# The last head of a Q·Kᵀ kernel stored in two halves, the first one by a scattering GpSimd DMA that leaves eight partitions to two small stores

## The chip, the cores and the metric

The kernel runs on one core of a Trainium2 chip. The metric is the device time of one execution in microseconds (us). Before the change it is 1061.1 us, the median of three runs (1060.9 to 1062.3).

A core has a matrix engine (TensorE, PE in the profile), a vector engine (DVE), a scalar engine (ACT), GpSimd (POOL) and a synchronisation engine (SP). Data moves between the memory outside the core (HBM, "dram" in names) and the on-chip memory SBUF by sixteen DMA engines, which work off queues. Here SP issues the stores and the early loads of q, ACT the other loads. Matrix products land in PSUM, from where ACT or DVE copies them to SBUF.

## What is computed

For each of 8 · 12 = 96 heads the kernel multiplies a 1024 x 64 matrix q with the transpose of a 1024 x 64 matrix k. The result is 96 matrices of 1024 x 1024 in 32-bit floats, 402.65 MB in all, against 50.33 MB of input.

```python
def reference(q: np.ndarray, k: np.ndarray) -> np.ndarray:
    return np.einsum('bhid,bhjd->bhij', q, k).astype(np.float32)
```

## The kernel before, in words

Synchronisation is written out by hand in one critical section, so the order of instructions on each engine is the order in which the Python code issues them. `Engine.run` (L33) gives an instruction its semaphore waits and one increment; `Landing.start` (L53) adds 16 to a semaphore when a DMA has landed.

Heads are worked through in blocks of 2, 2, 4, 8 and then five times 16 heads. While one block's products are computed, the next block's q and k are loaded (`load`, L153), cast to 16 bits by POOL (`cast_quads`, L201) and transposed by DVE (`transpose_quads`, L222). POOL's last cast and DVE's last transpose lie some 180 us ahead of the end, because the last block needs nothing prepared behind it.

For one head, `scores` (L256) makes 1024 rows of output. Output row 8p + t belongs to partition p and slot t, so a partition holds eight consecutive rows, 32 KB. For two slots at a time PE loads 128 columns of qT as weights and multiplies with kT in two matmuls of 512 columns each (L386), which fills one of two PSUM regions of 128 x 2048 floats. ACT copies the region into one of three output buffers `o_sb` (L288). After four such copies SP issues one store of 4 MB for the head (L301). A buffer is written again only when its store, three heads ago, has landed; ACT waits for that.

The last head (number 95, counted from 0) has a function of its own, `scores_uneven` (L307). It makes rows 0 to 127 first. The products run with only 32 columns of weights, and the result goes to the first 32 partitions of `x_sb`, the input buffer that is free by then: partition p holds rows 8p to 8p + 7, and only the first 16 partitions (rows 0 to 127) are used. ACT and DVE copy in turn (L338), and SP issues four stores of four partitions each (L359, issued in L380): partitions c, c+4, c+8 and c+12 for c = 0 to 3. Then come the rows 128 to 1023 on all 128 partitions, seven rows each, in an `o_sb` buffer; ACT alone makes the four copies, and SP issues one store of 3.5 MB (L372). At the very end SP waits for the semaphores of all stores (L513).

Of the kernel before, what the change touches and what calls it, by code (L numbers as in the profile page):

```python
# [5 lines left out]

F16 = mybir.dt.float16
F32 = mybir.dt.float32
P = 128


class Engine:
# [8 lines left out]
    def missing(self, events):  # L21
        want = {}
        for counter, value in events:
            if counter is not self and value > self.seen.get(counter, 0):
                want[counter] = max(value, want.get(counter, 0))
        self.seen.update(want)
        return list(want.items())

    def wait(self, events):
        for counter, value in self.missing(events):  # L30
# [29 lines left out]
def kernel(  # L60
# [6 lines left out]
    nc = tc.nc  # L67

    B, H, S, D = q.shape
    NT = S // P  # L70
    BH = B * H
# [7 lines left out]
    NMAX = max(sizes)  # L79
    CHUNK, HALVES = 64 * 32, 3  # L80
    TURNS = (3, 4, 5, 6, 10, 11, 12, 13)
    LOADS = {0: {}, 1: {}, 2: {1: 3}, 3: {2: 1}}

    pool = ctx.enter_context(tc.tile_pool(name="sb", bufs=1))
    psum = ctx.enter_context(
        tc.tile_pool(name="ps", bufs=1, space=bass.MemoryType.PSUM)
    )
    ident = pool.tile([P, P], F16, tag="ident")
    x_sb = pool.tile([P, NMAX * S * D // P], F32, name="x_sb", tag="x")
    half_sb = [pool.tile([P, CHUNK], F16, name=f"half{i}", tag=f"half{i}") for i in range(HALVES)]  # L90
    qk_sb = [
        [pool.tile([P, NMAX * S // 2], F16, name=f"{'qk'[x]}T{i}") for x in range(2)]
        for i in range(2)
    ]
    o_sb = [pool.tile([P, NT, S], F32, name=f"o_sb{i}", tag=f"out{i}") for i in range(3)]
    ps_all = psum.tile([P, 4 * S], F32, tag="po")

    ctx.enter_context(tc.tile_critical())

    pe = Engine(nc, nc.tensor, "pe_done")  # L100
    act = Engine(nc, nc.scalar, "act_done")
    dve = Engine(nc, nc.vector, "dve_done")
    gps = Engine(nc, nc.gpsimd, "pool_done")
    sp = Engine(nc, nc.sync, "sp_done")
# [18 lines left out]
    n, at = S * D // P * 2, 8 * S // 2  # L123
# [8 lines left out]
    input_busy = []  # L132
    outs = Ring(o_sb)
    input_landing = [Landing(nc, f"x{i}_in") for i in range(2)]
    tail_landing = Landing(nc, "tail_out")
    store_landing = {id(t): Landing(nc, f"out{i}_out") for i, t in enumerate(o_sb)}

    class Block:
# [165 lines left out]
            )  # L304
            out_busy.append(store_landing[id(buf)].start(dma))

        def scores_uneven(self, n, regions, w):  # L307
            half, g = divmod(n, self.N // 2)
            cs = slice(half * D, (half + 1) * D)
            qT = self.qk[0][cs, g * S : (g + 1) * S]  # L310
            kT = self.qk[1][cs, g * S : (g + 1) * S]
            head = of[self.first + n]
            Q, more, even = 32, NT, NT - 1
            few = P // more
            first = few * more

            def product(ps, slot, stationary, at, signal):
                m = stationary.shape[1]
                pe.run(lambda: load_weights(stationary, half * D, at), signal=False)
                for j in range(2):  # L320
                    col = slot * S + j * 512
                    done = pe.run(
                        lambda: multiply(
                            ps[0][at : at + m, col : col + 512],
                            stationary,
                            kT[:, j * 512 : (j + 1) * 512],
                            half * D,
                            at,
                        ),
                        ps[1],  # L330
                        signal=signal and j == 1,
                    )
                return done

            def evacuate(ps, done, dst, parts, N, events=(), by_dve=False):
                copier = dve if by_dve else act
                copied = copier.run(
                    lambda: (nc.vector.tensor_copy if by_dve else nc.scalar.copy)(  # L338
                        out=dst, in_=ps[0][:parts, : N * S]
                    ),  # L340
                    [*events, done],
                )
                ps[2].append(copied)
                return copied

            more_sb = x_sb[:Q, : more * S]
            written = []
            for t in range(0, more, w):
                ps = regions.next()
                for tt in range(w):  # L350
                    stationary = qT[:, t + tt :][:, : Q * more - more + 1 : more]
                    done = product(ps, tt, stationary, 0, tt == w - 1)
                dst = more_sb[:, t * S : (t + w) * S]
                by_dve = t // w % 2
                written.append(evacuate(ps, done, dst, Q, w, input_busy, by_dve))
            sp.wait(written)
            dst = head[:first].rearrange("(p t) j -> p (t j)", t=more)
            for c in range(4):
                self.store_part(sp, tail_landing, dst[c::4], more_sb[c:few:4])  # L359

            buf, out_free, _ = outs.next()
            rows = qT[:, first:].rearrange("c (m t) -> c t m", t=even)
            for t in range(0, even, w):
                ps = regions.next()
                N = min(w, even - t)
                for tt in range(N):
                    done = product(ps, tt, rows[:, t + tt], 0, tt == N - 1)
                dst = buf[:, t : t + N].rearrange("p t j -> p (t j)")
                copied = evacuate(ps, done, dst, P, N, out_free)
            self.over = [done]  # L370
            sp.wait([copied])
            self.store_part(  # L372
                sp,
                store_landing[id(buf)],
                head[first:].rearrange("(p t) j -> p (t j)", p=P),
                buf[:, :even].rearrange("p t j -> p (t j)"),
            )

        def store_part(self, eng, landing, dst, src):
            landing.start(eng.eng.dma_start(out=dst, in_=src))  # L380

    def load_weights(stationary, at, to=0):
        return nc.tensor.ldweights(stationary, tile_position=(at, to))  # L383

    def multiply(dst, stationary, moving, at, to=0):
        return nc.tensor.add_instruction(  # L386
            mybir.InstMatmult(
                name=nc.get_next_instruction_name(),
                ins=[nc.tensor.lower_ap(moving), nc.tensor.lower_ap(stationary)],
                outs=[nc.tensor.lower_ap(dst)],  # L390
                start_tensor_calc=True,
                stop_tensor_calc=True,
                ldweights=False,
                tile_position=(at, to),
                tile_size=(D, stationary.shape[1]),
            )
        )

    blocks, first = [], 0
# [6 lines left out]
    at = 0  # L406
# [24 lines left out]
    for x in range(2):  # L431
# [7 lines left out]
                out=ident,  # L439
                in_=ident,  # L440
                compare_op=mybir.AluOpType.not_equal,
                fill=1.0,
                base=0,
                pattern=[[-1, P]],
                channel_multiplier=1,
# [20 lines left out]
    def block(i, heads, regions, w):  # L466
        b = blocks[i]
        nxt = blocks[i + 1] if i + 1 < len(blocks) else None
        for n in heads:
            side = {}  # L470
            if nxt and nxt.by_pe:
                if n == 1:
                    side = {
                        u: [
                            lambda x=u // 2: nxt.transpose_rows(
                                x, regions.next(), dve, nc.vector.tensor_copy
                            )
                        ]
                        for u in (1, 3)
                    }  # L480
            elif nxt:
                parts = nxt.chunks()
                at = TURNS if i > EARLY else [m * b.N // len(parts) for m in range(len(parts))]
                some = [s for m, s in zip(at, parts) if m == n]
                side = {0: [lambda s=s: transposed(nxt, s) for s in some]}
            at = LOADS.get(i, {1: 1, 7: 1})
            if n in at:
                side[at[n]] = side.get(at[n], []) + [lambda: next_load(act)]
            if i == len(blocks) - 1 and n == b.N - 1:
                b.scores_uneven(n, regions, w)  # L490
            else:
                b.scores(n, side, regions, w)
            to_half(i + 2 + (n == b.N - 1))
# [16 lines left out]
    block(0, [1], halves_ps, 2)  # L510
    for i in range(1, len(blocks)):
        block(i, range(blocks[i].N), halves_ps, 2)
    sp.wait([(c, c.count) for c in [*store_landing.values(), tail_landing]])  # L513


# [28 lines left out]
```

## Time and profile before

| | |
|---|---|
| median of three runs | 1061.1 us (1060.9 to 1062.3) |
| the profiled execution's own time | 1061.62 us |
| its span, first to last instruction | 1059.8 us |
| moved by DMA | 453.21 MB, mean 428 GB/s |
| PE busy | 707.0 us (67%) |
| ACT busy | 699.9 us (66%) |
| DVE busy | 435.4 us (41%) |
| POOL busy | 354.0 us (33%) |
| store of one head, issue to landing | 21.7 us, 95 times |
| last store (3.5 MB), issue to landing | 15.7 us |

The profile lists groups of instructions with their busy time, the mean duration of one in nanoseconds, and the idle time ahead of them with what ended it. "SPq" is the queue of instructions that SP works through, DMA issues among them. The DMA share in a stretch of time is the mean busy share of the core's sixteen DMA engines; a packet is counted in the stretch in which it starts, so very short stretches are uneven. The trace also holds a record of every single DMA packet (start, duration, size), which the views only add up.

### The profile page before, as it was taken

Reading aid. Unit: us, or ns where it says so; the run is one execution under the profiler, and the core shown is the slowest. Engines: PE = TensorE matmul, PEld = TensorE weight load, DVE = VectorE, ACT = ScalarE, POOL = GpSimd, SP = SyncE. Lnnn points to the kernel's source line nnn. Section 1 sums busy time; section 2 is a strip of 40 time slices with the busy share of each in tenths; the row PEclk is TensorE's granted clock in tenths of the full one; section 3 lists DMA queues with packets and bytes.
Section 4 is the critical chain, followed back from the end, with each engine's and each line's share of the span. In section 5 each row is a group of like instructions: output and inputs, shape, how many; then the busy total and the mean of one; then the engine's idle time right before and its main releaser. Section 6 shows DMA issues by size and latency. Waiting matters only on the chain.

```text
span 1059.8 us, 3339 instructions
## 1 busy us (share of the span) xinstructions
PE 707.0 (67%) x1582; PEld 128.3 (12%) x807; DVE 435.4 (41%) x57; ACT 699.9 (66%) x388; POOL 354.0 (33%) x206
## 2 busy tenths in 40 slices
PE   6876744957477747557765756775574777777772
PEld 1111100101011101111110111111110111111110
DVE  2995939029193009439003907600670930000000
ACT  4766655857477737567856756775674778777772
POOL 7927465055380029064005509100913700000000
DMA  9999999999999999999999999999999999999997
GB/s 376 433 436 434 431 430 431 429 425 428 433 432 433 434 424 429 432 435 432 433 420 434 430 435 435 433 430 425 433 430 429 435 430 432 434 433 433 433 433 335
DMA packets 17041, 453.21 MB, mean 428 GB/s; under 512 B 1904, under 2 KB 1904, under 8 KB 2928
## 3 DMA queue, kind: packets, MB, share of 16 engines
q1 hardware_dynamic: 15008, 410.00, 89.9%
q10 hardware_dynamic: 2016, 42.99, 9.7%
q8 instruction: 9, 0.15, 0.0%
q14 instruction: 8, 0.07, 0.0%
HBM read 50.33 MB, written 402.65 MB: 427 GB/s over the span
## 4 chain that ended last, share of the span: by engine, by line
DMA 65%; ACT 16%; PE 8%; DVE 6%; POOL 4%; issue 1%; SPq 0%; ACTq 0%
DMA out_dram<-o_sb 60%; ACT o_sb L288 15%; PE ps_all L386 7%; DVE kT L230 4%; POOL half L211 3%; DMA x_sb<-in_k_dram 2%; DMA x_sb<-in_q_dram 2%; DVE qT L230 1%; DVE x_sb L338 0%; ACT o_sb L338 0%; DMA o_sb<-in_q_dram 0%; PE ps_all L244 0%; POOL qT L182 0%; DVE kT L251 0%; ACT kT L251 0%
## 5 line engine op out<-in xcount | busy, mean ns | idle before, releaser
L386 PE MATMUL ps_all<-kT,qT 64*128 64x512 f16 (+1 forms) x1550 | 702.9, 617 | 326.8 <-ACT o_sb L288 310.0
L288 ACT COPY o_sb<-ps_all 128x2048 f32<-128x2048 f32 (+1 forms) x380 | 687.5, 1859 | 330.5 <-DMA out_dram<-o_sb 288.3
L211 POOL CAST half<-x_sb 32x2048 f16<-32x2048 f32 x176 | 332.1, 1887 | 482.1 <-DMA x_sb<-in_q_dram 304.9
L230 DVE STREAM_TRANSPOSE qT<-half 128x2048 f16<-128x2048 f16 x22 | 202.6, 9477 | 270.8 <-POOL half L211 270.8
L230 DVE STREAM_TRANSPOSE kT<-half 128x2048 f16<-128x2048 f16 x22 | 202.3, 9525 | 134.8 <-POOL half L211 134.8
L383 PEld LDWEIGHTS <-qT 64*128 64x128 f16 (+1 forms) x775 | 125.2, 162 | 900.9 <-issue 882.2
L338 DVE COPY x_sb<-ps_all 32x2048 f32<-32x2048 f32 x2 | 4.6, 2280 | 175.5 <-PE ps_all L386 175.5
L230 DVE STREAM_TRANSPOSE kT<-kT 128x1024 f16<-128x1024 f16 x2 | 9.3, 4856 | 0.0
L230 DVE STREAM_TRANSPOSE qT<-qT 128x1024 f16<-128x1024 f16 x2 | 9.2, 4786 | 0.0
L211 POOL CAST qT<-o_sb 32x1024 f16<-32x1024 f32 x8 | 8.3, 1034 | 1.1 <-DMA o_sb<-in_q_dram 0.7
L211 POOL CAST kT<-o_sb 32x1024 f16<-32x1024 f32 x8 | 8.3, 1034 | 0.5
L338 ACT COPY o_sb<-ps_all 128x2048 f32<-128x2048 f32 (+1 forms) x4 | 6.4, 1658 | 2.7 <-PE ps_all L386 2.7
L251 DVE COPY qT<-ps_all 128x1024 f16<-128x1024 f16 x2 | 2.4, 1224 | 11.1 <-PE ps_all L244 11.1
L288 DVE COPY o_sb<-ps_all 128x1024 f32<-128x1024 f32 x4 | 4.9, 1224 | 4.4 <-PE ps_all L386 4.4
L244 PE MATMUL ps_all<-ident,qT 128*128 128x128 f16 x16 | 2.1, 311 | 6.8 <-POOL qT L182 6.7
L338 ACT COPY x_sb<-ps_all 32x2048 f32<-32x2048 f32 x2 | 3.7, 1854 | 2.1 <-PE ps_all L386 2.1
L251 ACT COPY kT<-ps_all 128x1024 f16<-128x1024 f16 x1 | 1.0, 1012 | 4.8 <-PE ps_all L244 4.8
L182 POOL CAST qT<-o_sb 128x512 f16<-128x512 f32 x4 | 2.3, 612 | 3.7 <-DMA o_sb<-in_q_dram 3.7
L251 ACT ACT_TABLE_LOAD x1 | 1.3, 1283 | 2.8 <-issue 2.8
L251 DVE COPY kT<-ps_all 128x1024 f16<-128x1024 f16 x1 | 1.2, 1224 | 4.4 <-PE ps_all L244 4.4
L182 POOL CAST kT<-o_sb 128x512 f16<-128x512 f32 x4 | 2.3, 613 | 0.5 <-DMA o_sb<-in_q_dram 0.5
L244 PE MATMUL ps_all<-ident,kT 128*128 128x128 f16 x16 | 2.0, 305 | 0.7 <-ACT o_sb L288 0.7
(8 smaller groups left out, 4.0 us busy)
## 6 DMA issues: line engine op xcount, KB each, us to landing
out_dram<-o_sb SPq DMA_DIRECT2D x95, 4096.0 KB, 21.7
x_sb<-in_q_dram ACTq DMA_DIRECT2D x5, 4096.0 KB, 24.9
x_sb<-in_k_dram ACTq DMA_DIRECT2D x5, 4096.0 KB, 23.7
out_dram<-o_sb SPq DMA_DIRECT2D x1, 3584.0 KB, 15.7
x_sb<-in_q_dram SPq DMA_DIRECT2D x1, 2048.0 KB, 14.7
x_sb<-in_k_dram SPq DMA_DIRECT2D x1, 2048.0 KB, 19.9
o_sb<-in_k_dram ACTq DMA_DIRECT2D x4, 256.0 KB, 5.0
o_sb<-in_q_dram SPq DMA_DIRECT2D x4, 256.0 KB, 5.2
```

Of the source, the lines that this page charges most:

```text
L182: lambda: nc.gpsimd.tensor_copy(out=rows[:, :, h], in_=self.raw[x][:, h * n : (h + 1) * n].rearrange("p (r d) -> p r d", d=D),),
L211: lambda: nc.gpsimd.tensor_copy(out=dst[q0 : q0 + 32].rearrange("p (r d) -> p r d", d=32), in_=raw[32 * b : 32 * b + 32, c * m : (c + 1) * ...
L230: lambda: nc.vector.transpose(out=dst, in_=buf.rearrange("p (r i) -> p r i", i=32)),
L244: lambda: nc.tensor.transpose(t_ps[:, t], rows[:, t], ident),
L251: lambda: copy(out=dst, in_=t_ps.rearrange("c t m -> c m t")), [done]
L288: lambda: (nc.vector.tensor_copy if by_dve else nc.scalar.copy)(out=dst, in_=ps[:, : w * S]),
L338: lambda: (nc.vector.tensor_copy if by_dve else nc.scalar.copy)(out=dst, in_=ps[0][:parts, : N * S]),
L383: return nc.tensor.ldweights(stationary, tile_position=(at, to))
L386: return nc.tensor.add_instruction(mybir.InstMatmult(name=nc.get_next_instruction_name(), ins=[nc.tensor.lower_ap(moving), nc.tensor.lower ...
```

## The change

Only the last head changes. It is made in two halves of 512 rows, by one function `part` for both: two products of two slots each, now with four rows to a partition (row 4p + t, 16 KB a partition), the first copied by ACT and the second by DVE.

Rows 0 to 511 go to all 128 partitions of `x_sb`. They are stored by one DMA that GpSimd issues, an indirect one: it reads for each partition, from a small integer tile `place_sb`, to which 16 KB row of the output that partition's data goes. The tile is computed on GpSimd (`places`): an iota gives each partition its row number, a copy turns it into floats, eight selects overwrite the numbers of partitions 16 to 19 and 48 to 51 by one that lies outside the output, and a copy turns it back to integers. The DMA is told that a number outside the bounds is no error: these partitions are skipped. GpSimd waits for itself between these small instructions (`settle`). The eight skipped partitions are stored by SP, in two plain DMAs of four partitions each, 64 KB a piece.

Rows 512 to 1023 go to an `o_sb` buffer in the same manner and are stored by SP in one DMA of 2 MB. The wait at the end has one semaphore more, that of the two small stores.

```diff
+    def settle(self):
+        self.eng.wait_ge(self.sem, self.count)
...
+    APART = (16, 48)
...
-        def scores_uneven(self, n, regions, w):
+        def scores_split(self, n, regions, w):
...
+            T = NT // 2
+            def part(rows, dst, events, copiers):
+                copied = []
+                for t in range(0, T, w):
+                    ps, ps_free, ps_busy = regions.next()
+                    for tt in range(w):
+                        stationary = rows[:, t + tt]
+                        pe.run(lambda: load_weights(stationary, half * D), signal=False)
+                        for j in range(2):
...
+                    copier = copiers[t // w]
+                    done = copier.run(
+                        lambda: (nc.vector.tensor_copy if copier is dve else nc.scalar.copy)(
+                            out=dst[:, t * S : (t + w) * S], in_=ps[:, : w * S]
                         ),
+                        [*events, done],
                     )
...
+            first = x_sb[:, : T * S]
+            rows = qT[:, : P * T].rearrange("c (m t) -> c t m", t=T)
+            copied = part(rows, first, input_busy, (act, dve))
+            index = self.places(first=(self.first + n) * S // T)
+            gps.wait([*copied, index])
+            tail_landing.start(
+                nc.gpsimd.indirect_dma_start(
+                    out=out.rearrange("b h (m t) j -> (b h m) (t j)", t=T),
+                    out_offset=bass.IndirectOffsetOnAxis(ap=place_sb, axis=0),
+                    in_=first,
+                    in_offset=None,
+                    bounds_check=BH * S // T - 1,
+                    oob_is_err=False,
                 )
+            )
+            sp.wait(copied)
+            for p in APART:
+                dst = head[p * T : (p + 4) * T].rearrange("(m t) j -> m (t j)", t=T)
+                self.store_part(sp, rest_landing, dst, first[p : p + 4])
...
+            second = buf[:, :T].rearrange("p t j -> p (t j)")
+            rows = qT[:, P * T :].rearrange("c (m t) -> c t m", t=T)
+            copied = part(rows, second, out_free, (act, dve))
+            sp.wait(copied)
             self.store_part(
                 sp,
                 store_landing[id(buf)],
-                head[first:].rearrange("(p t) j -> p (t j)", p=P),
-                buf[:, :even].rearrange("p t j -> p (t j)"),
-            )
+                head[P * T :].rearrange("(p t) j -> p (t j)", p=P),
+                second,
+            )
+        def places(self, first):
+            gps.settle()
+            gps.run(
+                lambda: nc.gpsimd.iota(
+                    place_sb, pattern=[[0, 1]], base=first, channel_multiplier=1
+                )
+            )
+            gps.settle()
+            gps.run(lambda: nc.gpsimd.tensor_copy(out=place_f, in_=place_sb))
+            for p in APART:
+                for i in range(4):
+                    gps.settle()
+                    gps.run(
+                        lambda: nc.gpsimd.affine_select(
+                            out=place_f,
+                            in_=place_f,
+                            compare_op=mybir.AluOpType.not_equal,
+                            fill=float(2 * BH * S),
+                            base=-(p + i),
+                            pattern=[[0, 1]],
+                            channel_multiplier=1,
+                        )
+                    )
+            gps.settle()
+            done = gps.run(lambda: nc.gpsimd.tensor_copy(out=place_sb, in_=place_f))
+            gps.settle()
+            return done
...
-    sp.wait([(c, c.count) for c in [*store_landing.values(), tail_landing]])
+    sp.wait([(c, c.count) for c in [*store_landing.values(), tail_landing, rest_landing]])
```

## The prediction

> **What bounds the kernel now.** The page first. Its DMA row is full in 39 of 40 slices, and most of ACT's idle time ends when a store lands: stores set the pace, and a head costs what 4 MB take.
>
> ```profile
> DMA  9999999999999999999999999999999999999997
> L288 ACT COPY o_sb<-ps_all 128x2048 f32<-128x2048 f32 (+1 forms) x380 | 687.5, 1859 | 330.5 <-DMA out_dram<-o_sb 288.3
> out_dram<-o_sb SPq DMA_DIRECT2D x95, 4096.0 KB, 21.7
> out_dram<-o_sb SPq DMA_DIRECT2D x1, 3584.0 KB, 15.7
> out_dram<-x_sb SPq DMA_DIRECT2D x4, 128.0 KB
> ```
>
> Then the timeline of the tail (start, duration): the four small stores go out from 1036.42 on, some 1.2 us each, the last store at 1042.86.
>
> ```profile
> 1028.05 1.85 ACT L338 COPY x_sb<-ps_all 32x2048 f32<-32x2048 f32 x1 [0.18 <-PE ps_all L386]
> 1029.82 2.28 DVE L338 COPY x_sb<-ps_all 32x2048 f32<-32x2048 f32 x1 [173.59 <-PE ps_all L386]
> ...
> 1036.42 4.67 SPq L380 DMA_DIRECT2D out_dram<-x_sb  x4
> ...
> 1038.28 4.55 ACT L338 COPY o_sb<-ps_all 128x2048 f32<-128x2048 f32 x3 [0.52 <-PE ps_all L386]
> ...
> 1042.86 0.34 SPq L380 DMA_DIRECT2D out_dram<-o_sb  x1
> ```
>
> SP's waits from 1036 us on: it waits 6.4 us for head 94 (landed 1049.6), 0.4 for the small stores, 8.4 for the last store. Nothing but transfers lies behind 1042.9.
>
> ```profile
> SPq L98 <- DMA out_dram<-o_sb: 8.4, 1, 8.4
> ...
> SPq L31 <- DMA out_dram<-o_sb: 6.4, 1, 6.4
> ...
> SPq L31 <- DMA out_dram<-x_sb: 0.4, 1, 0.4
> ```
>
> Last, DMA share by stretch of the tail (the last two columns are share and GB/s). A packet of 28 KB is 1.06 us, so a share of 0.07 in one us is one packet. From 1052 the engines run dry one after another, and one packet alone starts after 1057.
>
> ```profile
> 1048.00:1052.00 4.00, 0.00 (x0) 0.00 (x0) 0.00 (x0) 0.00 (x0) 0.00 (x0) 1.00 1.00 432
> 1052.00:1053.00 1.00, 0.00 (x0) 0.00 (x0) 0.00 (x0) 0.00 (x0) 0.00 (x0) 1.00 0.80 344
> 1053.00:1054.00 1.00, 0.00 (x0) 0.00 (x0) 0.00 (x0) 0.00 (x0) 0.00 (x0) 1.00 0.47 201
> 1054.00:1055.00 1.00, 0.00 (x0) 0.00 (x0) 0.00 (x0) 0.00 (x0) 0.00 (x0) 1.00 0.33 143
> 1055.00:1056.00 1.00, 0.00 (x0) 0.00 (x0) 0.00 (x0) 0.00 (x0) 0.00 (x0) 1.00 0.40 172
> 1056.00:1057.00 1.00, 0.00 (x0) 0.00 (x0) 0.00 (x0) 0.00 (x0) 0.00 (x0) 1.00 0.20 86
> 1057.00:1058.00 1.00, 0.00 (x0) 0.00 (x0) 0.00 (x0) 0.00 (x0) 0.00 (x0) 1.00 0.07 29
> ```
>
> **Sixteen strings of packets.** The packet records behind that view, strung end to start, give sixteen strings, one per DMA engine as I read them. A head's store is eight packets of 32 KB on each, 1.213 us apiece.
> - Four strings carry the small stores, four packets of 1.213 us each. They finish head 94 at 1042.93, 1043.25, 1044.48 and 1044.88, and their last packet at 1056.3, 1056.6, 1057.8 and 1058.2.
> - Three are late: head 94 at 1046.08, 1048.07, 1049.12, the end at 1054.6, 1056.5, 1057.6. The last one's packets run about 1.22 us all along: some 5% of 32 KB packets are over 1.216 us up to 1000 us, one engine's share. The middle one lost some 1.8 us near 979, where a 16 KB instruction packet ran.
> - Nine finish head 94 by 1045.0 and end by 1053.5.
>
> So the end, 1058.2, is set by an engine with extra packets. The mean end is 1054.65, thus 3.6 us is all that any division of the same bytes could give.
>
> **The change part by part.** An engine's end is its end of head 94 plus its packets, if they are queued in time.
>
> *Supply.* Copies keep their prices: ACT 128x2048 1.87 us, DVE 2.28 (timed on 32 partitions; its 128x1024 copies take 1.22, half, so I take 2.28). First half copied by 1032.10; the second follows in the steps of before's third and fourth copies, 1031.86 to 1033.7 on ACT (buffer free: head 92 landed near 1030.1) and 1034.05 to 1036.3 on DVE. SP's two small issues start at 1032.2, 0.75 and 1.25 us as before's; behind them waits only the last store, out at 1036.5, 6.4 us earlier. That is worth nothing at the end: the late strings are in head 94 until 1046 or later. Three early strings lose their idle of about 1 us, but end first.
>
> *Index tile.* Eleven small GpSimd operations, each 0.1 us (memset 128x1) to 1.9 us (the longest cast), and a round trip of its own semaphore each: 1 to 25 us. POOL is free from 842.8, 189 us ahead: nothing. A further instruction packet may cost one engine 0.3 us; 0, as 15 of 16 engines don't decide.
>
> *Issuing the scatter.* No GpSimd DMA is in the trace. Nearest rows: SP's issue, 0.33 to 1.28 us plus about 0.9 to the first packet; POOL's longest operation 1.9. Taken at 3 us, packets from 1035. Nothing is queued behind it on POOL but the end. The late string at 1048.07 has second-half packets until 1052.9, so only 18 us more would cost anything: nothing.
>
> *Packets.* Eight of 16 KB for each half, 0.607 us each (half of 1.213): 4.85 + 4.85 = 9.70 us, against 8.50 for eight of 28 KB. The small stores' strings have two of 0.607 instead of four of 1.213: 1044.88 + 1.21 + 9.70 = 1055.8, no longer the end. The scatter's price per byte is bounded by that rate from below and by the 2 KB packets of the first loads (84 ns against 76 at that rate, 1.11 times) from above if it is cut finer: 0 to 0.5 us; taken 0, as 16 KB load packets measured 0.608 to 0.615.
>
> *Whom it spares.* Late strings: 1046.08 + 9.70 = 1055.8; 1048.07 + 9.70 = 1057.8; 1049.12 + 9.76 = 1058.9. The eight skipped partitions are one string's share of a 128-partition store. If it is the last string's, its end is 1049.12 + 4.9 = 1054.0, and 1057.8 sets the end: 1057.77 - 1058.22 = -0.45 us. If not, 1058.88 - 1058.22 = +0.66. No view says which partitions that string serves. I take the first end: a choice and not a reading, resting only on the slowness being one engine's all along, which a fixed list of partitions can meet and a passing delay could not. Both ends stay in the range.
>
> The Trainium skill ("DMA: Bandwidth & Descriptors", The descriptor swizzle) puts partitions 16 to 19 and 48 to 51 on one engine, number 4; the same page (Latency and other measured facts) calls engines 7 and 15 usually the slower ones. By that rule the spared engine is not the slow one and the time would be rival A's; the trace agrees that one engine in sixteen is slow, and can't say which.
>
> *Sum.* Landing and wind-down behind the last packet stay (1.6 us; one semaphore more is 0.03). The profiled execution is 1061.62 us, 1.8 outside its span and 0.5 above the median: -0.45 gives 1061.17 there, **1060.6 us** against the median.
>
> **Rivals.**
> A. *The slow engine isn't spared*, and the change doesn't do what the skip suggests: +0.66, 1061.8. For it: twelve strings could be the spared one. Against: nothing in the trace; that its lateness is steady only says that a fixed list can meet it.
> B. *Slower: the scatter doesn't run like a head's store*, on fewer engines or in costlier packets. For it: before's stores of four partitions ran on four strings only. Against: stores of 128 partitions ran on all sixteen, and the scatter has 128. On eight engines each has sixteen packets of it: 1044.88 + 1.21 + 14.55 = 1060.6 for a small-store string, 1048.07 + 14.55 = 1062.6 for a late one; +2.4 to +4.4, say 1064.5. It decides (over 0.2%) from 1060.3 on, when the 1048.07 string's eight cost 1.5 times 4.85. The skill's page (Why a DMA increments its semaphore by 16 and not by 1) derives the number of engines from the outer sizes of both sides, sixteen for 128 and 24576; no row here shows it for a scatter, and by it B is not the time.
> C. *Faster*: the spared engine is the slow one, and the instruction packet near 979 falls elsewhere, so that the 1048.07 string is at 1046.3: 1046.3 + 9.70 = 1056.0, -2.2, 1058.8. Against: TensorE's instructions are the same up to there.
>
> **How the numbers follow.** 0.2% (2.1 us) is about what a measurement of this kernel can tell from no change. The forecast 0.36 (within, its own range 1060.1 to 1061.1), A 0.28 (within), B 0.25 (slower), C 0.11 (faster): faster 0.11, same 0.64, slower 0.25. Range 1058.8 (C) to 1064.2: outside lie the lower half of C and half of B, 0.18.
>
> **What would show it.** Right: the small stores go out near 1032, the last store near 1036.5, the landed semaphores by 1058.2, and the share falls later and more steeply, with two or three strings left after 1056. A shows one string alone at 1058.9. B shows more or fewer packets on the GpSimd queue than 120 of 16 KB, or a staircase beyond 1060. A span that ends early while the execution doesn't would be a cost outside these steps, and would make me wrong.

## The result, and the profile after

The changed kernel takes 1064.5 us (median of 20 runs, 1063.4 to 1066.8) where the kernel before, beside it, takes 1062.2 (20 runs, 1060.9 to 1065.0). The ratio is 1.0023, 95% interval 1.0016 to 1.0030: 2.4 us slower, just beyond the 0.2% that the prediction set as the bound. The forecast was 0.5 us faster, and the range ended at 1064.2. Those two were counted from 1061.1 us, three runs of the kernel before; beside the changed kernel it took 1.1 more. As a difference the 2.4 us lie inside the range (up to +3.1), but on the other side of zero than the forecast. The profiled execution of the changed kernel takes 1064.69 us, its span is 1062.9, so 1.8 us lie outside the span, as before.

First the page of the changed kernel: the DMA row, the copies of the other 95 heads, the GpSimd queue (q0: packets, MB, share), and the issues (count, KB each, us to landing).

```profile
DMA  9999999999999999999999999999999999999997
L296 ACT COPY o_sb<-ps_all 128x2048 f32<-128x2048 f32 (+1 forms) x380 | 687.6, 1859 | 331.1 <-DMA out_dram<-o_sb 287.5
q0 software_dynamic: 144, 1.97, 0.4%
out_dram<-o_sb SPq DMA_DIRECT2D x95, 4096.0 KB, 21.8
out_dram<-o_sb SPq DMA_DIRECT2D x1, 2048.0 KB, 24.5
out_dram<-x_sb SPq DMA_DIRECT2D x2, 64.0 KB
```

Up to head 94 nothing has changed: 21.8 us a store instead of 21.7, ACT waits as long as before. But the last store, though it has 2 MB instead of 3.5, takes 24.5 us to land instead of 15.7. It starts earlier and ends later. The 144 packets of q0 are 120 of 16 KB and 24 of four bytes.

The timeline of the tail (start, duration):

```profile
1028.74 1.87 ACT L344 COPY x_sb<-ps_all 128x2048 f32<-128x2048 f32 x1 [0.18 <-PE ps_all L420]
1030.51 2.29 DVE L344 COPY x_sb<-ps_all 128x2048 f32<-128x2048 f32 x1 [174.02 <-PE ps_all L420]
...
1032.89 1.44 SPq L414 DMA_DIRECT2D out_dram<-x_sb  x2
...
1033.81 1.16 POOL L359 DMA_INDIRECT out_dram<-x_sb,place  x1 [187.44 <-DVE x_sb L344]
...
1034.76 2.29 DVE L344 COPY o_sb<-ps_all 128x2048 f32<-128x2048 f32 x1 [1.95 <-PE ps_all L420]
...
1037.12 0.36 SPq L414 DMA_DIRECT2D out_dram<-o_sb  x1
```

Everything is issued by 1037.5, 5.7 us earlier than before (1043.2). So it is not the supply that is late. SP's waits from 1030 us on (total, times, longest; the three for DMAs shown):

```profile
SPq L35 <- DMA out_dram<-x_sb,place: 18.4, 1, 18.4
SPq L105 <- DMA out_dram<-o_sb: 4.8, 1, 4.8
...
SPq L35 <- DMA out_dram<-x_sb: 0.9, 1, 0.9
```

From 1037.5 on that is 18.4 us until the scatter has landed (1055.9), 0.9 for the small stores, and 4.8 for the last store (1061.6). The scatter and the small stores land late too, and then five engines still have packets of the last store, three of them beyond 1057.6. The DMA share and GB/s (last two columns) of the stretches show where the time went:

```profile
1048.00:1052.00 4.00, 0.00 (x0) 0.00 (x0) 0.00 (x0) 0.00 (x0) 0.00 (x0) 1.00 1.04 377
1052.00:1054.00 2.00, 0.00 (x0) 0.00 (x0) 0.00 (x0) 0.00 (x0) 0.00 (x0) 1.00 0.85 320
1054.00:1056.00 2.00, 0.00 (x0) 0.00 (x0) 0.00 (x0) 0.00 (x0) 0.00 (x0) 1.00 0.47 172
1056.00:1058.00 2.00, 0.00 (x0) 0.00 (x0) 0.00 (x0) 0.00 (x0) 0.00 (x0) 1.00 0.23 98
1058.00:1060.00 2.00, 0.00 (x0) 0.00 (x0) 0.00 (x0) 0.00 (x0) 0.00 (x0) 1.00 0.17 74
1060.00:1062.00 2.00, 0.00 (x0) 0.00 (x0) 0.00 (x0) 0.00 (x0) 0.00 (x0) 1.00 0.06 25
```

The first line is the one to learn from. The engines are full (1.04) and yet move 377 GB/s, where before's full stretch was 1.00 and 432. A share that stays while the bytes fall means that packets take longer than their size explains. The last two lines are the price: about three engines (0.17 of sixteen) are still busy from 1058 to 1060, and one on the mean from 1060 to 1062.

The packet records say which packets. (A string, as in the prediction, is the packets of one DMA engine put end to start.) All 16 KB packets of the tail take 0.61 us, the scatter's too (0.620 at most), but for two kinds (us, in order of time):

| packets of 16 KB | took | sum | at 0.61 |
|---|---|---|---|
| the eight of the two small stores | 1.62, 2.15, 1.68, 4.21, 4.06, 1.88, 2.67, 2.08 | 20.3 | 4.9 |
| eight of the last store, on the string that was late all along | 0.61, 1.03, 1.22, 1.22, 1.28, 1.13, 0.63, 0.61 | 7.7 | 4.9 |

The string that ends last, at 1061.29, had a small packet of 4.21 us (from 1049.53) and one of 2.08 (from 1054.36): 6.29 instead of 1.22. Without these 5.07 us it would have ended at 1056.2. Two more of the four small-store strings end at 1060.18 and 1060.78. The latest of the others end at 1057.55 and 1057.09.

### The profile page after: what moved, and what is told of

Read it like the earlier page. It is cut to its first block, busy times and chain, and to the rows that moved or that the text cites. A ratio compares the mean times of both kernels' runs of the same rounds, so it can differ in the third digit from the quotient of the medians.

```text
span 1062.9 us, 3336 instructions
## 1 busy us (share of the span) xinstructions
PE 700.7 (66%) x1568; PEld 127.3 (12%) x800; DVE 435.6 (41%) x57; ACT 693.6 (65%) x384; POOL 357.1 (34%) x218
## 4 chain that ended last, share of the span: by engine, by line
DMA 65%; ACT 15%; PE 7%; DVE 6%; POOL 4%; issue 1%; SPq 0%; ACTq 0%
DMA out_dram<-o_sb 60%; ACT o_sb L296 15%; PE ps_all L420 7%; DVE kT L238 4%; POOL half L219 3%; DMA x_sb<-in_k_dram 2%; DMA x_sb<-in_q_dram 2%; DVE qT L238 1%; DMA o_sb<-in_q_dram 0%; DVE x_sb L344 0%; DVE o_sb L344 0%; PE ps_all L252 0%; POOL qT L190 0%; DVE kT L259 0%; ACT kT L259 0%
## 5 line engine op out<-in xcount | busy, mean ns | idle before, releaser
L420 PE MATMUL ps_all<-kT,qT 64*128 64x512 f16 x1536 | 696.6, 617 | 326.6 <-ACT o_sb L296 310.0
L417 PEld LDWEIGHTS <-qT 64*128 64x128 f16 x768 | 124.2, 162 | 895.8 <-issue 876.1
L344 DVE COPY x_sb<-ps_all 128x2048 f32<-128x2048 f32 x1 | 2.3, 2293 | 174.0 <-PE ps_all L420 174.0
L344 DVE COPY o_sb<-ps_all 128x2048 f32<-128x2048 f32 x1 | 2.3, 2292 | 2.0 <-PE ps_all L420 2.0
## 6 DMA issues: line engine op xcount, KB each, us to landing
out_dram<-o_sb SPq DMA_DIRECT2D x95, 4096.0 KB, 21.8
x_sb<-in_k_dram ACTq DMA_DIRECT2D x5, 4096.0 KB, 24.5
out_dram<-o_sb SPq DMA_DIRECT2D x1, 2048.0 KB, 24.5
```

The lines of the kernel that those rows point to most:

```text
L344: lambda: (nc.vector.tensor_copy if copier is dve else nc.scalar.copy)(out=dst[:, t * S : (t + w) * S], in_=ps[:, : w * S]),
L420: return nc.tensor.add_instruction(mybir.InstMatmult(name=nc.get_next_instruction_name(), ins=[nc.tensor.lower_ap(moving), nc.tensor.lower ...
```

## The experiments

All eight leave the other 95 heads alone. A change of a few us in 1060 needs the interval, so all were timed in three or five rounds against the kernel before, whose median was 1062.1 us beside the first four runs and 1061.8 beside the others.

Theory: **a shared source**. In the kernel before, each small store read every fourth partition. In the changed kernel a small store reads four adjacent ones, 16 to 19 or 48 to 51, and these are also the late string's own eight partitions; so four strings fetch from one place beside its own string. (A place here is the eight partitions that one string serves in a store of 128 partitions. A packet's record does not name its partitions; whose place a packet reads is taken from the edit and the order of the shares.) Rivals: the packets wait because a GpSimd transfer runs beside them, or because of the rows that they write; the scatter itself costs what is missing.

**own_parts: the same small stores, other partitions read.** The destination, the sizes, the queue and the order of issue stay; the sources are every fourth partition, as before's were.

```diff
-                self.store_part(sp, rest_landing, dst, first[p : p + 4])
+                self.store_part(sp, rest_landing, dst, first[p - 16 : p : 4])
```

> The two small stores read partitions 0, 4, 8, 12 and 32, 36, 40, 44 instead of 16 to 19 and 48 to 51, into the same eight places of the output (so those 32 rows hold other rows' data). Theory 'shared source' (the eight partitions of one DMA string sit behind one path of about one engine's rate, and the four strings of the small stores plus the slow string itself squeeze through it): each of the eight small packets falls from 1.6 to 4.2 us to about 0.61 us, the end comes about 4 us earlier than in the changed kernel, that is 0.4 to 1.8 us faster than before. Rival 'destination' (stores of four partitions into 64 KB pieces are slow on the writing side, or because a GpSimd queue runs beside them): packets stay at 1 to 4 us, 2 to 3 us slower than before.

Measured: 1060.8 us, ratio 0.9991 (0.9982 to 0.9999). No 16 KB packet is over 0.64 us, and the last semaphore packet on any string ends at 1057.34 instead of 1061.30. The tail of own_parts, in the same columns:

```profile
1048.00:1052.00 4.00, 0.00 (x0) 0.00 (x0) 0.00 (x0) 0.00 (x0) 0.00 (x0) 1.00 0.99 422
1052.00:1054.00 2.00, 0.00 (x0) 0.00 (x0) 0.00 (x0) 0.00 (x0) 0.00 (x0) 1.00 0.79 336
1054.00:1056.00 2.00, 0.00 (x0) 0.00 (x0) 0.00 (x0) 0.00 (x0) 0.00 (x0) 1.00 0.25 107
1056.00:1058.00 2.00, 0.00 (x0) 0.00 (x0) 0.00 (x0) 0.00 (x0) 0.00 (x0) 1.00 0.06 25
1058.00:1060.00 2.00, 0.00 (x0) 0.00 (x0) 0.00 (x0) 0.00 (x0) 0.00 (x0) 1.00 0.00 0
```

Full engines move 422 GB/s again, and nothing is left after 1058. The packets wrote the same rows with the same scatter beside them, so neither of these stretches them: the choice of source partitions does.

**apart_parts: sources every fourth partition, but from 16 and 48 on.** Now each of the four strings reads from another string's place, and no two of them from the same.

```diff
-                self.store_part(sp, rest_landing, dst, first[p : p + 4])
+                self.store_part(sp, rest_landing, dst, first[p : p + 16 : 4])
```

> The small stores read partitions 16, 20, 24, 28 and 48, 52, 56, 60, again into the same places (wrong rows in them). 'Shared source': now each of the four strings reads where one other string reads, instead of four strings where a fifth reads: the small packets take 0.6 to 1.3 us, the time lies 1.5 us under to 0.3 us over before. 'Destination': unchanged packets of 1 to 4 us, 2 to 3 us slower than before.

Measured: 1061.2 us, ratio 0.9992 (0.9983 to 1.0001). Some 16 KB packets stretch, to between 0.67 and 1.24 us, about twice their price at most instead of seven times, some of the scatter's among them. So it isn't enough that a place is foreign; with one string beside the owner (the string whose place it is) the cost is small and spread, and the last semaphore packet ends at 1056.48.

**no_small: the small stores left out.**

```diff
-            sp.wait(copied)
-            for p in APART:
-                dst = head[p * T : (p + 4) * T].rearrange("(m t) j -> m (t j)", t=T)
-                self.store_part(sp, rest_landing, dst, first[p : p + 4])
```

> The changed kernel without its two small stores: 32 rows of the last head are not stored. Both theories on the small stores: the end is set by the second latest string, 0.5 to 1.9 us faster than before. Rival 'scatter' (the GpSimd DMA itself costs the time): still 1.5 us or more slower than before.

Measured: 1060.5 us, ratio 0.9989 (0.9979 to 0.9998). No packet is long, those of the late string neither, and the last semaphore packet ends at 1056.38. What own_parts still pays for its two small stores is within the intervals.

**no_skip: the scatter stores all 128 partitions, without small stores.**

```diff
-    APART = (16, 48)
+    APART = ()
...
-            sp.wait(copied)
-            for p in APART:
-                dst = head[p * T : (p + 4) * T].rearrange("(m t) j -> m (t j)", t=T)
-                self.store_part(sp, rest_landing, dst, first[p : p + 4])
```

> The scatter stores all 128 partitions, there are no small stores and no selects. Both theories on the small stores: the slow string isn't spared and sets the end, 0.3 to 1.0 us slower than before (0.66 by the working of the prediction's first rival). 'Scatter': 1.5 us or more slower.

Measured: 1062.6 us, ratio 1.0006 (0.9997 to 1.0015). One string ends alone at 1059.07, the next at 1055.65. In no_skip's windows that is a share near nothing which yet lasts:

```profile
1056.00:1058.00 2.00, 0.00 (x0) 0.00 (x0) 0.00 (x0) 0.00 (x0) 0.00 (x0) 1.00 0.08 33
1058.00:1060.00 2.00, 0.00 (x0) 0.00 (x0) 0.00 (x0) 0.00 (x0) 0.00 (x0) 1.00 0.02 8
```

This is rival A of the prediction as an experiment: the late string is not spared. Between no_skip and own_parts lies what sparing it is worth, 0.0015 of 1062 us = 1.6 us.

**plain_halves: two plain stores of 2 MB by SP, no scatter.**

```diff
-            index = self.places(first=(self.first + n) * S // T)
-            gps.wait([*copied, index])
-            tail_landing.start(
-                nc.gpsimd.indirect_dma_start(
...
             sp.wait(copied)
-            for p in APART:
-                dst = head[p * T : (p + 4) * T].rearrange("(m t) j -> m (t j)", t=T)
-                self.store_part(sp, rest_landing, dst, first[p : p + 4])
+            self.store_part(
+                sp, tail_landing, head[: P * T].rearrange("(p t) j -> p (t j)", p=P), first
+            )
```

> Two halves, both stored by SP with plain DMAs of 128 partitions; no scatter, no skip, no small stores. If the GpSimd DMA as such costs nothing: the same as the run in which the scatter stores all partitions, 0.3 to 1.0 us slower than before. If it costs something: faster than that run by its price.

Measured: 1062.8 us, ratio 1.0005 (0.9995 to 1.0014), the same as no_skip: within the intervals a scatter of 128 partitions costs no more than a plain store. One string ends alone again, at 1060.54, the next at 1057.06.

**spare_28: the scatter skips partitions 28 to 31 and 60 to 63 instead, without small stores.** It asks whether any list of eight partitions would have done.

```diff
-    APART = (16, 48)
+    APART = (28, 60)
...
-            sp.wait(copied)
-            for p in APART:
-                dst = head[p * T : (p + 4) * T].rearrange("(m t) j -> m (t j)", t=T)
-                self.store_part(sp, rest_landing, dst, first[p : p + 4])
```

> The changed kernel without small stores, and the scatter skips partitions 28 to 31 and 60 to 63 instead (their 32 rows are not stored). If the slow string is the one that serves partitions 16 to 19 and 48 to 51: it isn't spared, 0.3 to 1.0 us slower than before, as when nothing is skipped. If another list does as well: 0.5 to 1.9 us faster, as in the run without small stores.

Measured: 1063.2 us, ratio 1.0008 (0.9998 to 1.0017), against 0.9989 for no_small, which differs in the list alone. One string ends alone at 1059.57, the next at 1056.88. The late string is the one of partitions 16 to 19 and 48 to 51. The changed kernel's own trace says so as well: the scatter's eight four-byte packets for skipped partitions all lie on one string, the one that took 9.77 us for head 93 (1.22 a packet) where the others with undisturbed packets took 9.68, and that finished head 94 at 1049.80. The Trainium skill ("DMA: Bandwidth & Descriptors", Latency and other measured facts) calls engines 7 and 15 usually the slower ones; the cause that it guesses would hold only for DMAs issued by GpSimd, and the stores of the heads are SP's. By the same page (The descriptor swizzle) partitions 28 to 31 and 60 to 63 are engine 7's and 16 to 19 and 48 to 51 engine 4's. Here engine 4's partitions are the late ones (0.9989 when they are spared, 1.0008 when engine 7's are), and the measurement decides.

**before_adjacent: the kernel before, with adjacent partitions in its four small stores.** If the theory holds, it must be able to break the kernel that never had a scatter.

```diff
-                self.store_part(sp, tail_landing, dst[c::4], more_sb[c:few:4])
+                self.store_part(sp, tail_landing, dst[4 * c : 4 * c + 4], more_sb[4 * c : 4 * c + 4])
```

> The kernel before, with its four small stores taken over four adjacent partitions each (4c to 4c + 3) instead of every fourth one (c, c + 4, c + 8, c + 12); same bytes, same sixteen partitions, no GpSimd DMA. 'Shared source': the four strings of a small store now read from one source at a time, so 32 KB packets of 1.21 us stretch to between 2 and 5 us, and the end moves by 2 to 14 us. Rival (only the GpSimd queue beside them made small packets slow): packets stay at 1.21 us, within 0.3 us of before.

Measured: 1072.5 us (four runs), ratio 1.0102 (1.0083 to 1.0122), 10.7 us slower. The 32 KB packets of the small stores, 1.21 us in the kernel before, take up to 4.25 us. In the waits of before_adjacent the small stores take 9.1 us behind head 94, where the kernel before had 0.4:

```profile
SPq L31 <- DMA out_dram<-x_sb: 9.1, 1, 9.1
SPq L98 <- DMA out_dram<-o_sb: 8.4, 1, 8.4
...
SPq L31 <- DMA out_dram<-o_sb: 6.5, 1, 6.5
```

The windows show the same signature as the changed kernel. This is before_adjacent, a share of 1.11 (packets are counted where they start) for 403 GB/s:

```profile
1044.00:1048.00 4.00, 0.00 (x0) 0.00 (x0) 0.00 (x0) 0.00 (x0) 0.00 (x0) 1.00 1.11 403
```

And this is the kernel before, where 0.95 was enough for 408:

```profile
1044.00:1048.00 4.00, 0.00 (x0) 0.00 (x0) 0.00 (x0) 0.00 (x0) 0.00 (x0) 1.00 0.95 408
```

**respread: the theory used.** The scatter still skips the eight partitions. Their 32 rows are computed a second time into partitions 0 to 15, two rows to a partition (one of each group of sixteen), and stored by two DMAs of sixteen partitions with 4 KB each.

```diff
-            for p in APART:
-                dst = head[p * T : (p + 4) * T].rearrange("(m t) j -> m (t j)", t=T)
-                self.store_part(sp, rest_landing, dst, first[p : p + 4])
+            for i, p in enumerate(APART):
+                columns = qT[:, p * T : p * T + 32]
+                pe.run(lambda: load_weights(columns, half * D), signal=False)
...
+            again = x_sb[:32, T * S : T * S + 2 * S]
+            copied = act.run(
+                lambda: nc.scalar.copy(out=again, in_=ps[:32, : 2 * S]), [*input_busy, done]
+            )
...
+                self.store_part(
+                    sp,
+                    rest_landing,
+                    head[p * T : (p + 4) * T],
+                    again[:16, i * S : (i + 1) * S],
+                )
```

> The changed kernel, but the 32 rows of the skipped partitions are computed a second time (two products with 32 columns, one more copy of 32x2048 on ACT, 1.85 us) into partitions 0 to 15 and stored by two DMAs of sixteen partitions, 4 KB each, on all sixteen strings. 'Shared source': no packet waits behind partitions 16 to 19 or 48 to 51 but those of the string they belong to; each string gets 2 x 0.15 us more, at most about 1 us where four strings meet at the same source; the end is the second latest string's: 0.5 to 1.8 us faster than before. 'Destination' (what is left of it: extra stores beside a GpSimd DMA are slow): 1 us or more slower than before.

Measured: 1060.7 us, ratio 0.9988 (0.9979 to 0.9997), 1.2 us under the kernel before and some 3.7 under the changed one (1.0023 - 0.9988 = 0.0035). It computes all 96 heads and is faster than both. Some 16 KB packets still stretch, to 1.14 us at most, and its 4 KB packets from about 0.15 to 0.94, but the 128 KB lie on all sixteen strings and are read from four places instead of one; the last semaphore packet ends at 1057.26.

By how many strings read one place (the bytes count too: respread, in the last row, reads only a quarter of its 128 KB from each place):

| readers of a place | kernel | its long packets | ratio to before |
|---|---|---|---|
| its own string alone | own_parts, no_small | none | 0.9991, 0.9989 |
| its own and one more | apart_parts | 0.67 to 1.24 us (price 0.61) | 0.9992 |
| its own and four more, at most three of these at a time | the changed kernel | 1.0 to 4.2 us (price 0.61) | 1.0023 |
| four strings, one 4-partition store after another | before_adjacent | up to 4.25 us (price 1.21) | 1.0102 |
| four strings in each of four places, with 4 KB packets | respread | 0.64 to 1.14 us (price 0.61), 4 KB 0.19 to 0.94 (price 0.16) | 0.9988 |

What the runs show is that the source partitions decide, since own_parts changes nothing else. What it is between those partitions and the engines that is shared, no trace here names. The Trainium skill ("SBUF — State Buffer", Door 1: The DMA port swizzle) says that a DMA's bandwidth goes by how many of sixteen ports its partitions reach, and puts 16 to 19 and 48 to 51 on one port; the trace agrees: the four small-store strings on these partitions took 1.6 to 4.2 us for 16 KB, 2.6 to 6.9 times the 0.61 of own_parts' strings, which by that rule read from four ports.

## Why the prediction was wrong, point by point

- **Supply**: right. DVE's copy takes 2.29 us (2.28 taken), the small stores are issued at 1032.89 and 1033.27 (1032.2 expected), the last store at 1037.12 (1036.5). Being 5.7 us earlier shows no gain, as said. A side reading was off: two early strings had lost time idling (1.26 and 0.98 us), not three.
- **Index tile**: right. Its eleven operations take 0.13 to 0.19 us each and are done by 846 us, 187 us ahead.
- **Issuing the scatter**: the size was low, the verdict right. The first packet comes at 1038.86, 5.0 us after the instruction's start instead of 3, and 3.9 from the expected 1035. plain_halves and no_skip, 1.0005 and 1.0006, show that it costs nothing.
- **Packets, the scatter's**: right. 120 of 16 KB, eight on each of fifteen strings, 0.611 us each (0.620 at most), no extra price; the sixteenth string is the spared one.
- **Packets, the small stores'**: this is the step that failed. "The small stores' strings have two of 0.607 instead of four of 1.213: 1044.88 + 1.21 + 9.70 = 1055.8, no longer the end." The price was taken from packets that read every fourth partition, and put on packets of which four strings read the same eight, the late string's. They took 1.6 to 4.2 us. Nor was 0.61 the only price in sight: the prediction reads the 16 KB load packets as 0.608 to 0.615, but 41 of the 256 took over 0.65, up to 1.32. The string that ended last paid 6.29 us for its two instead of 1.21; its end was 1061.29, and taking the 5.07 us off gives 1056.2, near the 1055.8 worked out. Next in line would have been 1057.1 or so, so the failed step cost about 4.2 us of end. The diff showed it: `first[p : p + 4]` stands where `more_sb[c:few:4]` stood, and no bound was set for that difference.
- **Whom it spares**: the choice that rested on no view came out right, which was luck as far as its reasons go: they did not single out one string of sixteen. The late string is spared: no_skip at 1.0006 is where rival A put it (+0.66 us, measured +0.6), own_parts at 0.9991 and no_small at 0.9989 are near the forecast (-0.45 us, measured -1.0 and -1.2). But its relief was partly taken back: four foreign strings on its partitions stretched its own eight packets from 4.9 to 7.7 us.
- **Rival B** gave the right time, 1064.5, by luck: its mechanism did not happen, and its +3.4 us met a measured +2.4 on a start that was 1.1 higher. It priced the scatter on eight engines or in costlier packets; the scatter ran on fifteen and the spared one, at the price of a head's store. Its sentence "before's stores of four partitions ran on four strings only" looked at the right stores and asked only how many strings carry them, not what these strings read.
- **Rival C**: the instruction packet near 979 did not fall elsewhere (978.29 in the changed kernel). The string's loss there in the kernel before was 1.4 us by the packet records, not 1.8; only C used it.
- **What would show it**: the small and the last store went out early and a "staircase beyond 1060" came, which was B's sign; 120 packets of 16 KB, which was the forecast's. Both at once is what neither had in it.

## What to carry to other kernels

A packet's price holds for the partitions that it was measured on. When a DMA has few partitions, look which ones are read together: every fourth partition from 0 on cost these stores nothing, every fourth from 16 on up to twice the packet's price, and four adjacent ones up to seven times, with up to twice for the owner of the place. In a profile this shows as a DMA share that stays full while GB/s fall, and a leftover is better not read from the very place whose engine is to be relieved: here it paid to put it elsewhere first, even by computing it again (respread).

## What the runs showed of the hardware that was not expected

- A small store of four partitions is slowed far beyond a fair division: single 16 KB packets took 4.21 and 4.06 us. By the packet records no more than three small-store packets were under way at a time, so with the owner's that would be 4 x 0.61 = 2.4 us by equal shares. The owner's own 16 KB packets took 1.28 at most, and its 32 KB packets of head 94 stayed at 1.213 while two small ones beside them took 1.62 and 2.15. Why the owner comes off better, no run shows.
- Skipped partitions of the scatter do not vanish: each leaves a packet of four bytes (9 ns) on the engine that would have carried it. Eight of them, 120 data packets and 16 semaphore packets make the 144 of q0. They told which engine was spared.
- GpSimd's DMA had a lead of 5.0 us from its instruction (1033.81) to its first packet (1038.86), 3.9 of them after the instruction had ended.
- Issuing a store of four partitions took SP 0.33 us once and 1.06 the other time in the changed kernel, 0.75 and 1.23 in own_parts.
